# A 3x3 convolution with residual add: every engine runs in the written order, weight blocks first, packing of image n+2 ahead of the add of image n

## The chip, the cores and the metric

The kernel runs on one core of a Trainium2 chip. The metric is the device time of one execution in microseconds (us); smaller is better. Beside it stands a profile of one execution, whose span goes from the first to the last instruction that the profiler recorded on the core.

## What is computed

Sixteen images with 64 channels of 64x64 pixels are convolved with 64 filters of 64x3x3, with one pixel of zeros around each image, and a residual of the shape of the output is added. All arrays are float32.

```python
x_pad = np.pad(x, ((0, 0), (0, 0), (pad, pad), (pad, pad)), mode='constant')
for b in range(batch):
    for co in range(c_out):
        for ci in range(c_in):
            for kh in range(k):
                for kw in range(k):
                    output[b, co] += weight[co, ci, kh, kw] * x_pad[b, ci, kh:kh+h, kw:kw+w]
return (output + residual).astype(np.float32)
```

## The kernel before

**Loads.** Images are loaded in pairs (NPAIR = 8), each pair as 128 partitions (2 images x 64 channels) of 4096 pixels. `load_x(p)` (line 56) is issued by GpSimd (POOL) and converts x from float32 to bfloat16 on the way into `xr`, of which there are five buffers (NXR). The first five pairs are loaded at the start; pair p+5 is loaded when the packing has read pair p (line 100). The residual pairs go by SyncE (SP) into eight buffers `ro`, all issued at the start (line 63). The weights come by a DMA that ScalarE (ACT) issues (line 53).

**Weights.** VectorE (DVE) copies the weights once (line 72), so that they stand twice side by side; nine transposes on TensorE (PE) put them into a PSUM tile `tp` (line 76), and six copies on VectorE, which convert from float32 and are called casts here, set them as blocks into `wl` (line 88). `wl` is what every convolution matmul loads as weights.

**Packing.** Two output rows are computed at once: the 128 partitions of a packed image `xp` hold the odd rows of an image in the lower half and the even rows in the upper half. VectorE copies the even rows (line 97) and ScalarE the odd ones (line 98). There are four `xp` buffers, so the packing of an image must wait until the image four before has been convolved.

**Convolution and add.** An image takes 24 matmuls (3 kernel columns x 2 row offsets x 4 chunks of 8 row pairs, line 110), which accumulate in one PSUM tile `ps` of four banks. There are two such tiles, shared with `tp`, so image n+2 cannot start before image n has been added. Two instructions on VectorE (line 120), one for each row parity, add `ps` to the residual in `ro`, in place. When both images of a pair are done, SP stores the pair (line 123).

**What sets the order.** Each engine runs its instructions one after another in a fixed order. Here the programming framework chooses that order and sets the waits between engines; the order of the source is only its starting point. In the trace VectorE packs images 0 to 3 (line 97) before it casts the weights (line 88), although the casts stand ahead in the source, and after that it packs image n+4 after the add of image n. All DMAs share the core's 16 DMA engines; the profile lists the loads of x under queue q0, residual loads and stores under q1, the weights under q10.

Of the kernel before, what the change touches and what calls it, by code (L numbers as in the profile page):

```python
# [1 line left out]

# [5 lines left out]

FP32 = mybir.dt.float32
BF16 = mybir.dt.bfloat16  # L10
ADD = mybir.AluOpType.add


@with_exitstack
def kernel(
    ctx: ExitStack,
    tc: tile.TileContext,
    x: bass.AP,
    weight: bass.AP,
    residual: bass.AP,  # L20
    out: bass.AP,
):
    nc = tc.nc

    B, C, H, W = x.shape
    CO = weight.shape[0]
    K = weight.shape[2]
    assert C == 64 and CO == 64 and K == 3 and H == 64 and W == 64 and B == 16

    NPIX = H * W  # L30
    NPAIR = B // 2
    J = H // 2
    JC = 8
    NCHUNK = J // JC
    NXR = 5

    res_bc = residual.rearrange("b c h w -> (b c) (h w)")
    out_bc = out.rearrange("b c h w -> (b c) (h w)")
    x_bc = x.rearrange("b c h w -> (b c) (h w)")
    w_flat = weight.rearrange("co ci kh kw -> co (ci kh kw)")  # L40

    pool = ctx.enter_context(tc.tile_pool(name="pool", bufs=1))
    psum = ctx.enter_context(tc.tile_pool(name="psum", bufs=2, space=bass.MemoryType.PSUM))

    wdup = pool.tile([64, 2, 576], FP32)
    ident = pool.tile([64, 64], FP32)
    ro = [pool.tile([128, NPIX], FP32, name=f"ro{p}") for p in range(NPAIR)]
    xr = [pool.tile([128, NPIX], BF16, name=f"xr{i}") for i in range(NXR)]

    xp = [pool.tile([128, J + 1, W], BF16, name=f"xp{i}") for i in range(4)]  # L50
    wl = pool.tile([128, 2, 3, 2, 64], BF16)

    nc.scalar.dma_start(out=wdup[:, 0, :], in_=w_flat[:, :])

    def load_x(p):
        nc.gpsimd.dma_start(out=xr[p % NXR][:, :], in_=x_bc[128 * p : 128 * p + 128, :])  # L56

    load_x(0)
    make_identity(nc, ident[:, :])
    for p in range(1, NXR):  # L60
        load_x(p)
    for p in range(NPAIR):
        nc.sync.dma_start(out=ro[p][:, :], in_=res_bc[128 * p : 128 * p + 128, :])

    for t in xp:
        nc.vector.memset(t[0:64, 0, :], 0.0)  # L66
        nc.vector.memset(t[64:128, J, :], 0.0)  # L67
    nc.vector.memset(wl[0:64, 0, :, 1, :], 0.0)  # L68
    nc.vector.memset(wl[64:128, 1, :, 0, :], 0.0)  # L69


    nc.vector.tensor_copy(out=wdup[:, 1, :], in_=wdup[:, 0, :])  # L72
    wdup3 = wdup.rearrange("p d (ci t) -> p (d ci) t", t=9)
    tp = psum.tile([128, NCHUNK, JC, W], FP32, name="ps")
    for t in range(9):
        nc.tensor.transpose(out=tp[:, t // 8, t % 8, :], in_=wdup3[:, :, t], identity=ident[:, :])  # L76
    tpf = tp.rearrange("p c j w -> p (c j) w")

    for half, d, par, kh in (
        (0, 0, 0, 0),  # L80
        (1, 0, 0, 1),
        (1, 0, 1, 0),
        (0, 1, 0, 2),
        (0, 1, 1, 1),
        (1, 1, 1, 2),
    ):
        hp = slice(64 * half, 64 * half + 64)
        nc.vector.tensor_copy(out=wl[hp, d, :, par, :], in_=tpf[hp, 3 * kh : 3 * kh + 3, :])  # L88


    for p in range(NPAIR):
        o4 = ro[p].rearrange("q (j two w) -> q j two w", two=2, w=W)
        x4 = xr[p % NXR].rearrange("q (j two w) -> q j two w", two=2, w=W)
        for im in range(2):
            hp = slice(64 * im, 64 * im + 64)
            t = xp[(2 * p + im) % 4]
            nc.vector.tensor_copy(out=t[64:128, 0:J, :], in_=x4[hp, :, 0, :])  # L97
            nc.scalar.copy(out=t[0:64, 1 : J + 1, :], in_=x4[hp, :, 1, :])  # L98
        if p + NXR < NPAIR:
            load_x(p + NXR)  # L100
        for im in range(2):
            hp = slice(64 * im, 64 * im + 64)
            t = xp[(2 * p + im) % 4]
            ps = psum.tile([128, NCHUNK, JC, W], FP32, name="ps")
            order = [(1, 0), (1, 1), (0, 0), (0, 1), (2, 0), (2, 1)]
            for i, (kw, d) in enumerate(order):
                xlo, xhi = max(0, 1 - kw), min(W, W + 1 - kw)
                for c in range(NCHUNK):
                    j0 = JC * c
                    nc.tensor.matmul(  # L110
                        out=ps[:, c, :, xlo:xhi],
                        lhsT=wl[:, d, kw, :, :].rearrange("q r c -> q (r c)"),
                        rhs=t[:, j0 + d : j0 + d + JC, xlo + kw - 1 : xhi + kw - 1],
                        start=i == 0,
                        stop=i == len(order) - 1,
                        skip_group_check=True,
                    )
            psj = ps.rearrange("q c j w -> q (c j) w")
            for par in range(2):
                nc.vector.tensor_tensor(  # L120
                    out=o4[hp, :, par, :], in0=psj[64 * par : 64 * par + 64, :, :], in1=o4[hp, :, par, :], op=ADD
                )
        nc.sync.dma_start(out=out_bc[128 * p : 128 * p + 128, :], in_=ro[p][:, :])


# [1 line left out]
_INS = ['x', 'weight', 'residual']  # L127
_OUTS = [((16, 64, 64, 64), 'float32')]


# [23 lines left out]
```

## Time and profile before

| | |
|---|---|
| time, median of 3 runs | 129.42 us (128.45, 129.42 and 129.80) |
| time of the profiled execution | 128.27 us |
| its span | 126.4 us |
| mean granted TensorE clock | 0.963 |
| instructions | 994 |
| convolution matmuls, line 110 | 85.1 us busy, 377 of 384 recorded |
| adds, line 120 | 73.2 us busy, 32 of 2288 ns |
| packing, line 97 on VectorE | 11.0 us busy, 16 of 686 ns |
| packing, line 98 on ScalarE | 30.4 us busy, 16 of 1897 ns |
| casts of the weights, line 88 | 2.0 us busy, 6 of 352 ns |
| first convolution matmul | 28.66 us |
| chain that ended last | PE line 110 67%, DMA of x 19% |

The profiled execution's time is 1.87 us longer than its span; what lies around the span is outside the recorded instructions. Busy times of different engines overlap, so they don't add up to the span. "Idle before, releaser" in a row says how long the engine stood still just before that instruction, and what came last of the things it waited for. For a DMA the profile gives the time from issue to landing. A DMA queue's share is the time that its packets took, out of what 16 engines have in the span.

### The profile page before, as it was taken

The numbers are of one execution on the slowest core, as the hardware profiler recorded it, in microseconds if no ns is written. First come the engines' busy times: TensorE is split into PE (matmuls) and PEld (weight loads), VectorE is DVE, ScalarE is ACT, GpSimd is POOL, SyncE is SP. The second block draws the span as 40 slices with busy tenths as digits, with TensorE's granted clock in tenths as the row PEclk, the third lists the DMA queues.
The fourth block names the chain that finished last, engine by engine and source line by source line (L and its number), as shares of the span: only waits on it lengthen the run. The fifth ranks groups of instructions, "written<-read, shape, count | busy, mean of one in ns | idle before, by whom it ended". The sixth has DMA issues, their size and how long they took to land.

```text
span 126.4 us, 994 instructions
## 1 busy us (share of the span) xinstructions
PE 86.4 (68%) x386; PEld 38.3 (30%) x393; DVE 87.1 (69%) x65; ACT 31.6 (25%) x17; POOL 4.9 (4%) x14
## 2 busy tenths in 40 slices
PE   0003000009999999999999999999999999991000
PEld 0003000003444444444444444444444444440000
DVE  3001040063079999999999999999999989898500
ACT  4000083074060541506416144161441000000000
POOL 6300001001000010000000000000000000000000
PEclk9999999999999999999999999999999999999555
DMA  5999999999999999999999999999999999996193
GB/s 104 367 344 296 340 298 301 347 329 301 334 329 303 311 353 311 306 327 298 340 342 298 329 332 301 319 389 425 425 420 435 446 430 420 415 435 275 83 415 166
DMA packets 3540, 42.15 MB, mean 333 GB/s; under 512 B 400, under 2 KB 400, under 8 KB 464
## 3 DMA queue, kind: packets, MB, share of 16 engines
q1 hardware_dynamic: 2304, 33.56, 63.5%
q0 software_dynamic: 1152, 8.39, 31.7%
q10 hardware_dynamic: 80, 0.15, 0.3%
q8 instruction: 3, 0.05, 0.1%
q14 instruction: 1, 0.01, 0.0%
HBM read 33.70 MB, written 16.78 MB: 399 GB/s over the span
## 4 chain that ended last, share of the span: by engine, by line
PE 67%; DMA 19%; DVE 3%; DVEq 2%; issue 1%; POOL 0%; POOLq 0%
PE ps L110 67%; DMA xr<-in_x_dram 19%; DVEq L149 2%; DVE ro L120 2%; DVE xp L97 1%; DVE wl L88 1%; POOL xr L56 0%; POOL ident masks.py:197 0%; POOLq L138 0%
## 5 line engine op out<-in xcount | busy, mean ns | idle before, releaser
L110 PE MATMUL ps<-xp,wl 128*128 128x504 bf16 (+1 forms) x377 | 85.1, 384 | 16.4 <-DVE wl L88 16.0
L120 DVE TENSOR_TENSOR ro<-ps,ro 64x2048 f32<-64x2048 f32 x32 | 73.2, 2288 | 8.0 <-PE ps L110 7.5
L110 PEld LDWEIGHTS <-wl 128*128 128x128 bf16 x384 | 37.2, 99 | 64.0 <-DVE wl L88 16.4
L98 ACT COPY xp<-xr 64x2048 bf16<-64x2048 bf16 x16 | 30.4, 1897 | 62.3 <-PE ps L110 32.5
L97 DVE COPY xp<-xr 64x2048 bf16<-64x2048 bf16 x16 | 11.0, 686 | 13.7 <-DMA xr<-in_x_dram 13.5
L76 PE MATMUL ps<-ident,wdup 64*128 64x64 f32 x9 | 1.3, 320 | 11.4 <-DVE wdup L72 11.4
L72 DVE COPY wdup<-wdup 64x576 f32<-64x576 f32 x1 | 0.5, 452 | 8.7 <-DMA wdup<-in_weight_dram 8.7
L56 POOL DMA_DIRECT2D xr<-in_x_dram x8 | 4.4, 556 | 42.0 <-ACT xp L98 25.4
L76 PEld LDWEIGHTS ps<-ident,wdup 64*128 64x128 f32 x9 | 1.1, 205 | 11.4 <-issue 11.4
L88 DVE CAST wl<-ps 64x192 bf16<-64x192 f32 x6 | 2.0, 352 | 0.1
L98 ACT ACT_TABLE_LOAD x1 | 1.3, 1283 | 1.3 <-PEq L138 1.3
L66 DVE MEMSET xp<- 64x32 uint32 x4 | 0.3, 85 | 0.9 <-PEq L138 0.8
L67 DVE MEMSET xp<- 64x32 uint32 x4 | 0.3, 85 | 0.2
masks.py:199 POOL TENSOR_SCALAR_AFFINE_SELECT ident<-ident 64x64 f32<-64x64 f32 x1 | 0.3, 258 | 0.1
L69 DVE MEMSET wl<- 64x96 uint32 x1 | 0.1, 138 | 0.1
L68 DVE MEMSET wl<- 64x96 uint32 x1 | 0.1, 138 | 0.1
masks.py:197 POOL MEMSET ident<- 64x64 f32 x1 | 0.2, 170 | 0.0
L138 POOL MEMSET const-float32-0.0<- 128x1 f32 x1 | 0.1, 103 | 0.2 <-issue 0.2
L138 POOL MEMSET const-bfloat16-1.0<- 128x1 bf16 x1 | 0.1, 106 | 0.0
L138 POOL MEMSET const-uint8-127<- 128x1 uint8 x1 | 0.1, 106 | 0.0
L138 POOL MEMSET const-float32-1.0<- 128x1 f32 x1 | 0.1, 103 | 0.0
## 6 DMA issues: line engine op xcount, KB each, us to landing
ro<-in_residual_dram SPq DMA_DIRECT2D x8, 2048.0 KB, 43.2
out_dram<-ro SPq DMA_DIRECT2D x8, 2048.0 KB, 23.0
xr<-in_x_dram POOLq DMA_DIRECT2D x8, 1024.0 KB, 40.9
wdup<-in_weight_dram ACTq DMA_DIRECT2D x1, 144.0 KB, 10.1
```

Source lines behind the costliest of these rows:

```text
L56: nc.gpsimd.dma_start(out=xr[p % NXR][:, :], in_=x_bc[128 * p : 128 * p + 128, :])
L66: nc.vector.memset(t[0:64, 0, :], 0.0)
L67: nc.vector.memset(t[64:128, J, :], 0.0)
L72: nc.vector.tensor_copy(out=wdup[:, 1, :], in_=wdup[:, 0, :])
L76: nc.tensor.transpose(out=tp[:, t // 8, t % 8, :], in_=wdup3[:, :, t], identity=ident[:, :])
L88: nc.vector.tensor_copy(out=wl[hp, d, :, par, :], in_=tpf[hp, 3 * kh : 3 * kh + 3, :])
L97: nc.vector.tensor_copy(out=t[64:128, 0:J, :], in_=x4[hp, :, 0, :])
L98: nc.scalar.copy(out=t[0:64, 1 : J + 1, :], in_=x4[hp, :, 1, :])
L110: nc.tensor.matmul(out=ps[:, c, :, xlo:xhi], lhsT=wl[:, d, kw, :, :].rearrange("q r c -> q (r c)"), rhs=t[:, j0 + d : j0 + d + JC, xlo + k ...
L120: nc.vector.tensor_tensor(out=o4[hp, :, par, :], in0=psj[64 * par : 64 * par + 64, :, :], in1=o4[hp, :, par, :], op=ADD)
L138: nc = _bacc.Bacc("TRN2", target_bir_lowering=False, num_devices=1)
L149: with _tile.TileContext(nc) as tc:
```

## The change

The source is regrouped into functions, and the whole body is put under `tc.manual_schedule()`: every engine then gets its instructions in the order in which they are written. The written order is this: the loads, the zero fills, the copy, transposes and casts of the weights; then the packing of images 0 and 1; then for each image n its convolution, the packing of image n+2, and the add of image n. `load_x(p + 5)` is issued after the packing of the second image of pair p, and the store of a pair after the add of its second image. Shapes, buffers, engines and the number of instructions stay.

```diff
-    nc.scalar.dma_start(out=wdup[:, 0, :], in_=w_flat[:, :])
-
     def load_x(p):
         nc.gpsimd.dma_start(out=xr[p % NXR][:, :], in_=x_bc[128 * p : 128 * p + 128, :])
 
-    load_x(0)
-    make_identity(nc, ident[:, :])
-    for p in range(1, NXR):
-        load_x(p)
-    for p in range(NPAIR):
+    def load_ro(p):
         nc.sync.dma_start(out=ro[p][:, :], in_=res_bc[128 * p : 128 * p + 128, :])
...
+    def pack(n):
+
+        p, im = divmod(n, 2)
+        hp = slice(64 * im, 64 * im + 64)
+        x4 = xr[p % NXR].rearrange("q (j two w) -> q j two w", two=2, w=W)
+        t = xp[n % 4]
+        nc.vector.tensor_copy(out=t[64:128, 0:J, :], in_=x4[hp, :, 0, :])
+        nc.scalar.copy(out=t[0:64, 1 : J + 1, :], in_=x4[hp, :, 1, :])
+        if im == 1 and p + NXR < NPAIR:
+            load_x(p + NXR)
+
+    def convolve(n):
+        t = xp[n % 4]
+        ps = psum.tile([128, NCHUNK, JC, W], FP32, name="ps")
...
+        return ps
+
+    def add(n, ps):
+        p, im = divmod(n, 2)
+        hp = slice(64 * im, 64 * im + 64)
+        o4 = ro[p].rearrange("q (j two w) -> q j two w", two=2, w=W)
+        psj = ps.rearrange("q c j w -> q (c j) w")
+        for par in range(2):
+            nc.vector.tensor_tensor(
+                out=o4[hp, :, par, :], in0=psj[64 * par : 64 * par + 64, :, :], in1=o4[hp, :, par, :], op=ADD
+            )
+        if im == 1:
+            nc.sync.dma_start(out=out_bc[128 * p : 128 * p + 128, :], in_=ro[p][:, :])
 
+    with tc.manual_schedule():
+        nc.scalar.dma_start(out=wdup[:, 0, :], in_=w_flat[:, :])
+        load_x(0)
+        make_identity(nc, ident[:, :])
+        for p in range(1, NXR):
+            load_x(p)
+        for p in range(NPAIR):
+            load_ro(p)
...
+        nc.vector.tensor_copy(out=wdup[:, 1, :], in_=wdup[:, 0, :])
...
+        for t in range(9):
+            nc.tensor.transpose(out=tp[:, t // 8, t % 8, :], in_=wdup3[:, :, t], identity=ident[:, :])
...
+            nc.vector.tensor_copy(out=wl[hp, d, :, par, :], in_=tpf[hp, 3 * kh : 3 * kh + 3, :])
+
+        pack(0)
+        pack(1)
+        for n in range(B):
+            ps = convolve(n)
+            if n + 2 < B:
+                pack(n + 2)
+            add(n, ps)
```

The zero fills and the matmuls inside `convolve` are those of before, in the same order.

More of the change, by code (lines that the diff above doesn't have):

```diff
@@ L51 @@
     wl = pool.tile([128, 2, 3, 2, 64], BF16)
-    nc.scalar.dma_start(out=wdup[:, 0, :], in_=w_flat[:, :])
     def load_x(p):
         nc.gpsimd.dma_start(out=xr[p % NXR][:, :], in_=x_bc[128 * p : 128 * p + 128, :])
-    load_x(0)
-    make_identity(nc, ident[:, :])
-    for p in range(1, NXR):
-        load_x(p)
-    for p in range(NPAIR):
[L63 to L88, printed above, removed]
@@ L91 @@
-    for p in range(NPAIR):
-        o4 = ro[p].rearrange("q (j two w) -> q j two w", two=2, w=W)
[L93 to L123, printed above, removed]
@@ new lines, in convolve @@
+    def convolve(n):
+        t = xp[n % 4]
+        ps = psum.tile([128, NCHUNK, JC, W], FP32, name="ps")
+        order = [(1, 0), (1, 1), (0, 0), (0, 1), (2, 0), (2, 1)]
+        for i, (kw, d) in enumerate(order):
+            xlo, xhi = max(0, 1 - kw), min(W, W + 1 - kw)
+            for c in range(NCHUNK):
+                j0 = JC * c
+                nc.tensor.matmul(
+                    out=ps[:, c, :, xlo:xhi],
+                    lhsT=wl[:, d, kw, :, :].rearrange("q r c -> q (r c)"),
+                    rhs=t[:, j0 + d : j0 + d + JC, xlo + kw - 1 : xhi + kw - 1],
+                    start=i == 0,
+                    stop=i == len(order) - 1,
+                    skip_group_check=True,
+                )
+        return ps
@@ new lines, in add @@
+    def add(n, ps):
+        p, im = divmod(n, 2)
+        hp = slice(64 * im, 64 * im + 64)
+        o4 = ro[p].rearrange("q (j two w) -> q j two w", two=2, w=W)
+        psj = ps.rearrange("q c j w -> q (c j) w")
+        for par in range(2):
+            nc.vector.tensor_tensor(
+                out=o4[hp, :, par, :], in0=psj[64 * par : 64 * par + 64, :, :], in1=o4[hp, :, par, :], op=ADD
+            )
+        if im == 1:
+            nc.sync.dma_start(out=out_bc[128 * p : 128 * p + 128, :], in_=ro[p][:, :])
@@ new lines @@
+    with tc.manual_schedule():
[6 more added lines that the diff above has]
+            load_ro(p)
+        for t in xp:
+            nc.vector.memset(t[0:64, 0, :], 0.0)
+            nc.vector.memset(t[64:128, J, :], 0.0)
+        nc.vector.memset(wl[0:64, 0, :, 1, :], 0.0)
+        nc.vector.memset(wl[64:128, 1, :, 0, :], 0.0)
+        nc.vector.tensor_copy(out=wdup[:, 1, :], in_=wdup[:, 0, :])
+        wdup3 = wdup.rearrange("p d (ci t) -> p (d ci) t", t=9)
+        tp = psum.tile([128, NCHUNK, JC, W], FP32, name="ps")
+        for t in range(9):
+            nc.tensor.transpose(out=tp[:, t // 8, t % 8, :], in_=wdup3[:, :, t], identity=ident[:, :])
+        tpf = tp.rearrange("p c j w -> p (c j) w")
+        for half, d, par, kh in (
+            (0, 0, 0, 0),
+            (1, 0, 0, 1),
+            (1, 0, 1, 0),
+            (0, 1, 0, 2),
+            (0, 1, 1, 1),
+            (1, 1, 1, 2),
+        ):
+            hp = slice(64 * half, 64 * half + 64)
+            nc.vector.tensor_copy(out=wl[hp, d, :, par, :], in_=tpf[hp, 3 * kh : 3 * kh + 3, :])
[6 more added lines that the diff above has]
+            add(n, ps)
```

## The prediction

> **What bounds the kernel now.** I read the page first: engine busy times, the 40 slices, the DMA queues. No compute engine is above 69%, yet the DMA row is full from the second slice on and breaks only near the end.
>
> ```profile
> PE 86.4 (68%) x386; PEld 38.3 (30%) x393; DVE 87.1 (69%) x65; ACT 31.6 (25%) x17; POOL 4.9 (4%) x14
> DMA  5999999999999999999999999999999999996193
> q1 hardware_dynamic: 2304, 33.56, 63.5%
> q0 software_dynamic: 1152, 8.39, 31.7%
> q10 hardware_dynamic: 80, 0.15, 0.3%
> HBM read 33.70 MB, written 16.78 MB: 399 GB/s over the span
> ```
>
> Queue q0 carries x (converted to bf16 on the way: 8.39 MB are written for 16.78 MB read), q1 the residual loads and the stores. Together their packets fill 95.2% of the 16 engines' 126.4 us. The kernel is close to a stream of 50.48 MB with gaps, so the second view is the DMA queues from 5 to 81 us, while both loads run.
>
> ```profile
> q0 software_dynamic: 1102, 8.11, 50.9%
> q1 hardware_dynamic: 1109, 16.07, 50.5%
> ```
>
> The two queues share evenly. Counted as read, x is 16.22 MB, q1 16.07, the weights 0.15: 32.4 MB in 76 us, 427 GB/s. The third view is busy time by stretch (columns: stretch, length, PE, PEld, DVE, ACT, POOL, clock, DMA share, GB/s), at the end of the kernel.
>
> ```profile
> 86.00:100.00 14.00, 13.89 (x63) 6.02 (x64) 13.90 (x9) 3.79 (x2) 0.00 (x0) 1.00 1.00 430
> 114.00:115.00 1.00, 0.17 (x1) 0.00 (x0) 0.79 (x1) 0.00 (x0) 0.00 (x0) 1.00 0.95 410
> 115.00:116.00 1.00, 0.00 (x0) 0.00 (x0) 1.00 (x1) 0.00 (x0) 0.00 (x0) 1.00 0.58 246
> 116.00:117.00 1.00, 0.00 (x0) 0.00 (x0) 0.99 (x2) 0.00 (x0) 0.00 (x0) 1.00 0.19 82
> 117.00:118.00 1.00, 0.00 (x0) 0.00 (x0) 1.00 (x1) 0.00 (x0) 0.00 (x0) 0.56 0.00 0
> 118.00:119.00 1.00, 0.00 (x0) 0.00 (x0) 0.80 (x1) 0.00 (x0) 0.00 (x0) 0.50 0.00 0
> 119.00:120.00 1.00, 0.00 (x0) 0.00 (x0) 0.00 (x0) 0.00 (x0) 0.00 (x0) 0.50 0.62 262
> ```
>
> Stores alone run at the same rate (430) until about 115. Then the engines run dry until the last store is issued. Idle from 115 to 120: 0.42+0.81+1+1+0.38 = 3.6 us. That hole is all that an earlier compute chain can win from the stream. The fourth view, the timeline, shows why that chain is late (columns: start, length, engine, line, operation; in brackets the idle time before and its releaser).
>
> ```profile
> 11.41 1.26 PE L76 MATMUL ps<-ident,wdup 64*128 64x64 f32 x9 [11.41 <-DVE wdup L72]
> 16.33 3.82 ACT L98 COPY xp<-xr 64x2048 bf16<-64x2048 bf16 x2 [13.74 <-DMA xr<-in_x_dram]
> 26.17 1.41 DVE L97 COPY xp<-xr 64x2048 bf16<-64x2048 bf16 x2 [8.43 <-DMA xr<-in_x_dram]
> 27.61 2.01 DVE L88 CAST wl<-ps 64x192 bf16<-64x192 f32 x6
> 28.66 16.61 PE L110 MATMUL ps<-xp,wl 128*128 128x512 bf16 x68 [15.99 <-DVE wl L88]
> 35.59 4.59 DVE L120 TENSOR_TENSOR ro<-ps,ro 64x2048 f32<-64x2048 f32 x2 [5.96 <-PE ps L110]
> 51.48 4.59 DVE L120 TENSOR_TENSOR ro<-ps,ro 64x2048 f32<-64x2048 f32 x2
> 61.33 0.69 DVE L97 COPY xp<-xr 64x2048 bf16<-64x2048 bf16 x1
> 62.05 4.59 DVE L120 TENSOR_TENSOR ro<-ps,ro 64x2048 f32<-64x2048 f32 x2
> 103.81 4.59 DVE L120 TENSOR_TENSOR ro<-ps,ro 64x2048 f32<-64x2048 f32 x2 [0.33 <-PE ps L110]
> 114.21 4.59 DVE L120 TENSOR_TENSOR ro<-ps,ro 64x2048 f32<-64x2048 f32 x2 [0.60 <-PE ps L110]
> ```
>
> The transposes end at 12.67 and image 0 is packed by 16.33+1.91 = 18.24. But VectorE has the six weight casts behind the packing of images 2 and 3, whose x lands only at 26.17. So PE, ready from 18.24, waits 16 us in all and begins at 28.66. From there VectorE sets the pace: two adds (4.59) and a copy (0.69) make 5.28 with their gaps (62.05-51.48 = 10.57 for two images).
>
> **The change, part by part.** No instruction is added or removed, and each engine issues the same kinds and counts. Only orders differ, so every price below is a shift.
>
> *Weight casts to the front.* They run from 12.67 to 14.7, 1.6 us before x0 lands at 16.33: hidden. Were that cover gone, each us of delay would push packing by one. PE now waits for ScalarE's half of image 0 and starts at 18.25, 10.4 earlier. Image 0 takes 35.59-28.66 = 6.93 as before, so it ends at 25.2.
>
> *Packing of image n+2 ahead of the add of image n.* This adds a wait: VectorE's first add now stands behind the packing of image 2, which waits for x1 at 26.17. The add begins at 26.17+0.69+0.03 = 26.89 instead of 25.2; that is 1.7 us of the 10.4 given back. PE feels it too: image 2 needs the PSUM buffer of image 0, free at 26.89+4.59 = 31.48, where PE would be ready at 25.2+5.28 = 30.5. After that the two engines march at 5.28.
>
> Each later even packing has a due time, 0.72 ahead of its add, and its x must have landed by then. The landings are read from the issue to landing times and the timeline:
>
> ```profile
> 57.03 1.90 ACT L98 COPY xp<-xr 64x2048 bf16<-64x2048 bf16 x1 [3.94 <-DMA xr<-in_x_dram]
> 36.00 1.90 ACT L98 COPY xp<-xr 64x2048 bf16<-64x2048 bf16 x1 [6.01 <-DMA xr<-in_x_dram]
> 30.28 0.53 POOL L56 DMA_DIRECT2D xr<-in_x_dram  x1 [9.31 <-ACT xp L98]
> 46.65 0.53 POOL L56 DMA_DIRECT2D xr<-in_x_dram  x1 [15.84 <-DVE xp L97]
> xr<-in_x_dram POOLq DMA_DIRECT2D x1, 1024.0 KB, 39.4
> ```
>
> x2 lands at 36.00 and is due at 26.89+2x5.28-0.72 = 36.7; x4 at 57.03, due 57.9; x7 at 46.65+39.4 = 86.05, due 89.5. The covers are 0.7, 0.8 and 3.4 us: thin but positive, so I cost these waits at nothing. Every us lost there delays all later adds by one.
>
> *The DMAs moved with it.* POOL issues x6 after the packing of image 3 (31.5+0.7 = 32.2 instead of 30.28) and x7 after that of image 5 (about 42.8 instead of 46.65). Queue q0 still holds x3 and x4 until 57, so it never runs empty and landings stay. SP issues the stores some 8.5 us earlier, behind the residual loads in the same queue.
>
> *The end.* The add of image 13 starts at 26.89+13x5.28 = 95.5 (103.81 before). The last two are paced by PE, 114.21-103.81 = 10.40 for two: 105.9, ending at 110.5. So the last store is issued at 110.5, 8.3 us earlier than 118.8. It then lies behind the store before it:
>
> ```profile
> 93.69 4.59 DVE L120 TENSOR_TENSOR ro<-ps,ro 64x2048 f32<-64x2048 f32 x2
> 108.43 10.72 SPq L123 DMA_DIRECT2D out_dram<-ro  x2
> out_dram<-ro SPq DMA_DIRECT2D x1, 2048.0 KB, 14.5
> out_dram<-ro SPq DMA_DIRECT2D x1, 2048.0 KB, 9.2
> out_dram<-ro SPq DMA_DIRECT2D x1, 2048.0 KB, 6.3
> ```
>
> These are the landing times of the sixth, seventh and eighth store. The sixth is issued at 93.69+4.59 = 98.3 and lands at 112.8; the seventh lands at 108.43+9.2 = 117.6. A store in a full queue thus takes 4.8 to 4.9 (2.10 MB at 430 is 4.88). The last one, alone, lands at 118.8+6.3 = 125.1. Queued, it lands at 117.6+4.9 = 122.5.
>
> **The sum.** 10.4 (PE start) less 1.7 (first add behind x1) less 0.4 (pace) is 8.3 on the compute chain; of it 2.6 arrive at the end (125.1-122.5), because the stream cannot be emptied sooner. Span 126.4-2.6 = 123.8, time 128.27-2.6 = 125.7 against the profiled execution's own 128.27. The bounds of the gain: from below 1.2, if the queued store still costs its 6.3 behind 117.6; from above 3.6, the whole idle hole, if the engines that finish late catch up. A floor: 50.48 MB at 427 GB/s are 118.2 us, with 1.1 ahead of the first packet and 2.2 behind the last, a span of 121.5 and a time of 123.4. I take 4.9 since it is the spacing of stores that were queued as this one will be.
>
> The profiled execution is the lowest seen; the median shown is 129.42, and the four times together have a middle of 128.9, 0.7 above it. Half of that I carry: 126.0.
>
> By the Trainium skill, "DMA: Bandwidth & Descriptors", section "Where 436 GB/s comes from", transfers between HBM and SBUF are bound by the HBM side at about 358 GB/s. By that rule the last store would take an estimated 5.9 in the queue, the gain would be 1.6 and the profiled time 126.7. This trace disagrees: 430 GB/s for 14 us of stores.
>
> **The rivals.** *The last store costs as much queued as alone.* Then it lands at 117.6+6.3 = 123.9: gain 1.2, time 127.1 on the profiled scale, within 1%. For it speaks that the tail of the seventh store was uneven (share 0.58, then 0.19), so a slow engine may hold the last packets. Against it, the spacing of the sixth and seventh.
>
> *The compute chain sets the end.* If the stream could run faster, the store issued at 110.5 would land 6.3 later, at 116.8: gain 8.3, time 120.0. It needs the stream's remaining bytes nearly six us sooner; no stretch of the load stage beats 427 by so much. Against.
>
> *Slower: the earlier stores take x's share.* If the stores issued from 36.8 on ran beside the residual loads and not behind them, x would have a third of the stream. The five loads after x2 (10.5 MB) at 142 GB/s would take 74 us, x7 would land at 110, and the last store is issued 21.0 after x7 (110.5-89.5): 131, time 140.5. It decides from x7 at 99.1 on (time 129.6). Against it: in the trace the stores do queue behind.
>
> ```profile
> L63 SPq DMA_DIRECT2D ro<-in_residual_dram x8: 328/454/822, 0.7 to 10.9; - x8
> out_dram<-ro SPq DMA_DIRECT2D x1, 2048.0 KB, 43.0
> ro<-in_residual_dram SPq DMA_DIRECT2D x1, 2048.0 KB, 70.3
> 45.54 73.61 SPq L123 DMA_DIRECT2D out_dram<-ro  x8
> ```
>
> The first store, issued at 45.54, lands at 88.5, after the last residual load (issued 10.9, landed 81.2).
>
> **How the numbers follow.** Forecast 0.76, the store as dear as alone 0.12, compute sets the end 0.06, x starved 0.06. The time is the forecast's, 126.0. The range reaches down to the floor, 123.4, and up to 128.0: the bound of 127.1 with the 0.7 between the profiled run and the middle, rounded up. About 1% is what a measurement of this kernel can tell from no change. Faster by over 1% is the forecast, the compute rival, less a little for a forecast that runs high: 0.80; within 1%, 0.14; slower, 0.06.
>
> **What would show it.** Right: the casts directly after the transposes; the first convolution matmul near 18.3; the first add near 26.9, released by the copy behind x1; adds 5.28 apart; the last store issued between 110 and 112 and landing about 4.9 after the one before; DMA full until about 121. Wrong: an x landing that holds an add by several us in mid-kernel, stores that land ahead of residual loads, a hole in the DMA row before the last store, or a stream above 435 GB/s over long stretches.

## The result

The changed kernel takes 125.37 us (median of 4 runs, 125.34 to 125.41). The kernel before took 129.18 beside it (4 runs, 128.45 to 129.80). The ratio is 0.971, with a 95% interval of 0.965 to 0.976: 2.9% faster. In the three later comparisons below the kernel before had medians of 128.46 to 128.74, against which the gain would be nearer 2.5%. The profiled execution takes 125.34 with a span of 123.6 (before 128.27 and 126.4).

From the page of the changed kernel, the DMA slices and the two large queues (packets, MB, share of 16 engines):

```profile
DMA  5999999999999999999999999999999999999990
q1 hardware_dynamic: 2304, 33.56, 64.8%
q0 software_dynamic: 1152, 8.39, 32.4%
```

The packets and bytes are the same as before, but the hole is gone: the row is full to the second-last slice, and the shares rise because the span has shrunk around the same work (97.2% after 95.2%).

The timeline of the changed kernel (start, length, engine, line, operation, idle before and releaser):

```profile
12.52 2.02 DVE L132 CAST wl<-ps 64x192 bf16<-64x192 f32 x6 [1.41 <-PE ps L121]
16.19 3.82 ACT L66 COPY xp<-xr 64x2048 bf16<-64x2048 bf16 x2 [13.60 <-DMA xr<-in_x_dram]
18.14 12.27 PE L78 MATMUL ps<-xp,wl 128*128 128x512 bf16 x48 [5.65 <-ACT xp L66]
26.00 0.69 DVE L65 COPY xp<-xr 64x2048 bf16<-64x2048 bf16 x1 [8.40 <-DMA xr<-in_x_dram]
26.71 4.59 DVE L94 TENSOR_TENSOR ro<-ps,ro 64x2048 f32<-64x2048 f32 x2
31.45 28.82 PE L78 MATMUL ps<-xp,wl 128*128 128x512 bf16 x126 [1.04 <-DVE ro L94]
106.22 4.59 DVE L94 TENSOR_TENSOR ro<-ps,ro 64x2048 f32<-64x2048 f32 x2 [0.74 <-PE ps L78]
```

The casts run at 12.52 and PE starts at 18.14, released by ScalarE's packing, 10.5 earlier than before. The first add waits for the packing of image 2, which waits for x1 (the second pair of images). PE pays 1.04 for that at image 2. The last add ends at 110.8 (before 118.8). The issues of the last two stores, and their times to landing:

```profile
100.72 10.46 SPq L98 DMA_DIRECT2D out_dram<-ro  x2
out_dram<-ro SPq DMA_DIRECT2D x1, 2048.0 KB, 16.7
out_dram<-ro SPq DMA_DIRECT2D x1, 2048.0 KB, 11.4
```

The seventh store lands at 100.72+16.7 = 117.4, where it landed before (117.6), although it was issued 7.7 earlier: it stood in the queue. The eighth lands at 110.8+11.4 = 122.2, 4.8 after it (before 125.1). Busy time by stretch at the end (the last two columns are DMA share and GB/s):

```profile
114.00:115.00 1.00, 0.00 (x0) 0.00 (x0) 0.00 (x0) 0.00 (x0) 0.00 (x0) 0.50 1.03 442
119.00:120.00 1.00, 0.00 (x0) 0.00 (x0) 0.00 (x0) 0.00 (x0) 0.00 (x0) 0.50 0.92 393
120.00:121.00 1.00, 0.00 (x0) 0.00 (x0) 0.00 (x0) 0.00 (x0) 0.00 (x0) 0.50 0.39 164
121.00:122.00 1.00, 0.00 (x0) 0.00 (x0) 0.00 (x0) 0.00 (x0) 0.00 (x0) 0.50 0.12 49
```

All compute engines have been done since 110.8, and the stream alone runs on for 11 us. So the compute chain moved by 8.0 and the end by 2.9: the rest of the chain's gain is spent waiting for the stream.

### The profile page after: what moved, and what is told of

It is laid out like the page before. It is cut to its first block, busy times and chain, and to the rows that moved or that the text cites. A ratio compares the mean times of both kernels' runs of the same rounds, so it can differ in the third digit from the quotient of the medians.

```text
span 123.6 us, 995 instructions
## 1 busy us (share of the span) xinstructions
PE 87.9 (71%) x386; PEld 38.1 (31%) x393; DVE 87.6 (71%) x65; ACT 31.6 (26%) x17; POOL 5.0 (4%) x14
## 4 chain that ended last, share of the span: by engine, by line
PE 60%; DMA 19%; DVE 6%; DVEq 2%; issue 2%; POOL 1%; POOLq 0%
PE ps L78 60%; DMA xr<-in_x_dram 19%; DVE ro L94 6%; DVEq L166 2%; POOL xr L54 1%; POOL ident masks.py:199 0%; POOL ident masks.py:197 0%; DVE xp L65 0%; POOLq masks.py:199 0%; POOLq L155 0%
## 5 line engine op out<-in xcount | busy, mean ns | idle before, releaser
L78 PE MATMUL ps<-xp,wl 128*128 128x504 bf16 (+1 forms) x377 | 86.6, 385 | 7.1 <-ACT xp L66 5.7
L65 DVE COPY xp<-xr 64x2048 bf16<-64x2048 bf16 x16 | 11.0, 689 | 10.5 <-DMA xr<-in_x_dram 10.0
```

The lines of the kernel that those rows point to most:

```text
L78: nc.tensor.matmul(out=ps[:, c, :, xlo:xhi], lhsT=wl[:, d, kw, :, :].rearrange("q r c -> q (r c)"), rhs=t[:, j0 + d : j0 + d + JC, xlo + k ...
```

## The experiments

The theory: the weight casts at the front carry the gain, and the DMA stream caps it, as long as the last store is issued before the stream runs dry. The rivals: the packing order carries it; or the time follows the compute chain. Where a measured ratio is given, it is to the kernel before on the same chip. The changed kernel itself was timed only in the comparison above, so a difference from its 125.37 is one between comparisons; three of the kernels below that differ little from it took 125.27 to 125.42.

**The casts back behind the packing of images 0 to 3.**

```diff
-        for half, d, par, kh in (
...
-            nc.vector.tensor_copy(out=wl[hp, d, :, par, :], in_=tpf[hp, 3 * kh : 3 * kh + 3, :])
-        pack(0)
-        pack(1)
+        for n in range(4):
+            pack(n)
+        for half, d, par, kh in (
...
+            nc.vector.tensor_copy(out=wl[hp, d, :, par, :], in_=tpf[hp, 3 * kh : 3 * kh + 3, :])
         for n in range(B):
             ps = convolve(n)
-            if n + 2 < B:
+            if n >= 2 and n + 2 < B:
```

> The written order is kept, but images 0 to 3 are packed ahead of the weight casts on VectorE, as in the kernel before; from image 4 on, packing of n+2 stays ahead of the add of n. Theory (the casts carry the gain): the first convolution matmul goes back to 28.5, the first add to 35.4, the last store to about 118.6, the hole in the DMA row is there again, time 127.6 to 128.9. Rival (the packing order carries the gain): the last store is issued by 112 and the time stays at 125.3 to 126.5.

Measured: 129.66 (8 runs, 128.80 to 130.55), ratio 1.008 (1.005 to 1.012). The gain is gone, so the casts carry it. The timeline of the longest of the eight runs:

```profile
28.07 2.02 DVE L134 CAST wl<-ps 64x192 bf16<-64x192 f32 x6
29.13 87.41 PE L78 MATMUL ps<-xp,wl 128*128 128x512 bf16 x377 [15.99 <-DVE wl L134]
37.23 4.59 DVE L94 TENSOR_TENSOR ro<-ps,ro 64x2048 f32<-64x2048 f32 x2 [7.14 <-PE ps L78]
116.57 4.59 DVE L94 TENSOR_TENSOR ro<-ps,ro 64x2048 f32<-64x2048 f32 x2 [0.74 <-PE ps L78]
```

The time is longer than expected (127.6 to 128.9), with the last store at 121.2 and not 118.6 in this profile. PE starts 0.5 later than in the profile before (29.13 against 28.66). The first image takes 37.23-29.13 = 8.1 and not 6.93 (taken up below). And the adds go 5.29 apart on average (79.34 us for 15) where the kernel before had 5.24 (78.62). Where the chain sets the end, the written order thus costs some 0.7 us by these two profiles; it does not help.

**Packing four ahead, behind the add, casts at the front.**

```diff
-        pack(0)
-        pack(1)
+        for n in range(4):
+            pack(n)
         for n in range(B):
             ps = convolve(n)
-            if n + 2 < B:
-                pack(n + 2)
             add(n, ps)
+            if n + 4 < B:
+                pack(n + 4)
```

> The casts stay at the front; the packing goes back to the order that the trace of the kernel before shows: images 0 to 3 first, then image n+4 behind the add of image n. Theory (the DMA stream sets the end as long as the last store is issued before the stream runs dry at 114 to 116): the packing of image 4 waits on VectorE for x2 at 35.85 and holds the add of image 1 until 36.6, so the compute chain runs 4.4 late and the last store is issued at 115.0 to 115.6, yet the time is only 125.2 to 126.3. Rival (the time follows the compute chain): 4.4 more, 129.7.

Measured: 125.27 (4 runs, 125.10 to 126.38), ratio 0.977 (0.971 to 0.983). The time is that of the changed kernel. With this run all four combinations have been measured: with the casts at the front both packing orders gain, and with the casts late the new packing order gains nothing. The profile is of the longest of the four runs, and its compute chain is several us later. The timeline, and the clock by stretch (PE, PEld, DVE, ACT, POOL, then clock, DMA share, GB/s):

```profile
35.88 0.69 DVE L65 COPY xp<-xr 64x2048 bf16<-64x2048 bf16 x1 [3.79 <-DMA xr<-in_x_dram]
36.60 4.59 DVE L94 TENSOR_TENSOR ro<-ps,ro 64x2048 f32<-64x2048 f32 x2
41.34 70.94 PE L78 MATMUL ps<-xp,wl 128*128 128x512 bf16 x306 [3.75 <-DVE ro L94]
112.32 4.59 DVE L94 TENSOR_TENSOR ro<-ps,ro 64x2048 f32<-64x2048 f32 x2 [0.60 <-PE ps L78]
```

```profile
42.00:44.00 2.00, 2.00 (x6) 0.73 (x5) 2.00 (x1) 0.00 (x0) 0.53 (x1) 0.50 0.97 287
44.00:46.00 2.00, 2.00 (x7) 0.60 (x6) 1.99 (x2) 0.27 (x1) 0.00 (x0) 0.50 0.96 336
```

The add of image 1 begins at 36.60, as expected, behind x2. But PE, standing still for 3.75 us, comes back at half clock, which was not expected (the mean clock of this run is 0.936, of the other three 0.947 to 0.964). The last store is issued at 116.9 and not at 115.0 to 115.6, just past the point where the stream runs dry, and this run takes 126.38. So the order in which images are packed is of use after all: not for the time in itself, but because it has the last store issued at 110.8, some 4 us ahead of that point (in this run the DMA share falls to 0.54 from 115 to 116).

**Packing directly behind the add.**

```diff
-            if n + 2 < B:
-                pack(n + 2)
             add(n, ps)
+            if n + 2 < B:
+                pack(n + 2)
```

> As the changed kernel, with the packing of image n+2 directly behind the add of image n and not ahead of it. Theory (stream): the first add starts at 25.1 and no longer waits for x1, adds follow 5.3 to 5.4 apart, the last store is issued between 109 and 110.5, and the time stays at 125.2 to 125.5. Rival (the time follows the compute chain): 1 to 1.7 less, 123.6 to 124.3. Rival (the place ahead of the add is what keeps PE fed): PE waits for packing in each image, the last store after 114, time above 126.

Measured: 125.28 (4 runs, 125.12 to 125.48), ratio 0.975 (0.971 to 0.980).

```profile
25.15 4.59 DVE L94 TENSOR_TENSOR ro<-ps,ro 64x2048 f32<-64x2048 f32 x2 [7.50 <-PE ps L78]
30.61 10.57 PE L78 MATMUL ps<-xp,wl 128*128 128x512 bf16 x47 [0.30 <-DVE xp L65]
106.24 4.59 DVE L94 TENSOR_TENSOR ro<-ps,ro 64x2048 f32<-64x2048 f32 x2 [0.64 <-PE ps L78]
```

The first add no longer waits for x1 (25.15). The 1.6 us won are lost again to a wait of 0.3 on packing at every second image, so the last store is issued at 110.9, where it was, a little later than expected. The time is the same: whether the packing stands ahead of the add or behind it makes no difference to it.

**One store left out, then two, and one in the kernel before.**

```diff
-        if im == 1:
+        if im == 1 and p != 0:
             nc.sync.dma_start(out=out_bc[128 * p : 128 * p + 128, :], in_=ro[p][:, :])
```

The second has `p > 1` there; the third has `if p != 0:` ahead of the store in the kernel before.

> As the changed kernel, without the store of the first pair (2.10 MB of 50.48 MB leave the stream; the first two output images are not written). Theory (stream): the compute chain is the same, last store issued at 110.8, but the queue ahead of it is 4.9 shorter, it lands at 117.1 to 117.5, time 120.2 to 120.7. Rival (compute chain sets the end): the time stays at 125.3.

> As the changed kernel, without the stores of the first two pairs (4.19 MB less; the first four output images are not written). Theory: with one store left out the stream was just as long as the compute chain; with two the chain sets the end: last store issued at 110.8, landing 6.3 later at 117.1, time 119.9 to 120.3, so the second store left out brings 0.3 at most. Rival (the stream is still the bound): 115.2 to 115.6.

> The kernel before, without the store of the first pair (2.10 MB less in the stream; the first two output images are not written). Theory (there the compute chain sets the end and the stream waits for it): the last store is issued at 118 to 120 as before, the hole in the DMA row ahead of it grows from 3.6 to about 8.5, and the time stays in the spread of the kernel before, 127.8 to 129.8. Rival (the stream bounded the kernel before as well): 4.9 less, 123.4 to 124.4.

Measured: one store out 120.16 (4 runs), ratio 0.936 (0.932 to 0.940); two out 120.12 (2 runs, 120.10 and 120.14), ratio 0.934 (0.927 to 0.941); the kernel before with one out 128.40 (8 runs, 128.02 to 129.23), ratio 0.999 (0.996 to 1.003). In the changed kernel one store less is worth 5.2 us and the next one nothing. In the kernel before even the first is worth nothing. The stretches around the last store show why, with one store out, with two out, and in the kernel before with one out:

```profile
108.00:110.00 2.00, 0.00 (x0) 0.00 (x0) 1.99 (x2) 0.00 (x0) 0.00 (x0) 0.75 0.94 401
110.00:112.00 2.00, 0.00 (x0) 0.00 (x0) 0.92 (x1) 0.00 (x0) 0.00 (x0) 0.50 0.73 311
```

```profile
106.00:108.00 2.00, 0.40 (x2) 0.00 (x0) 1.56 (x1) 0.00 (x0) 0.00 (x0) 1.00 0.35 147
108.00:110.00 2.00, 0.00 (x0) 0.00 (x0) 1.99 (x2) 0.00 (x0) 0.00 (x0) 0.91 0.00 0
```

```profile
106.00:108.00 2.00, 2.00 (x11) 0.89 (x10) 1.99 (x2) 0.00 (x0) 0.00 (x0) 1.00 0.08 33
108.00:110.00 2.00, 2.00 (x11) 0.93 (x10) 1.39 (x2) 0.00 (x0) 0.00 (x0) 1.00 0.13 57
...
116.00:118.00 2.00, 0.00 (x0) 0.00 (x0) 1.99 (x2) 0.00 (x0) 0.00 (x0) 1.00 0.00 0
```

With one store out the stream is nearly as short as the chain (share 0.73 while the last store is issued). With two it stands idle and waits. That puts numbers to both limits: the changed kernel's compute chain alone would allow 120.1, its stream 125.4.

**Stores on a queue of their own.**

```diff
-            nc.sync.dma_start(out=out_bc[128 * p : 128 * p + 128, :], in_=ro[p][:, :])
+            nc.scalar.dma_start(out=out_bc[128 * p : 128 * p + 128, :], in_=ro[p][:, :])
```

> As the changed kernel, with the stores issued by ScalarE on its own queue instead of SyncE behind the residual loads. Theory (the slower rival of the prediction, made true: queues share the stream evenly, so x gets a third while stores and residual loads run): x3 lands near 50, x7 between 100 and 110, adds wait for it, time 132 to 140, with a stream that runs dry at the end. Rival (only the sum of bytes counts, whichever queue carries them): 125.2 to 126.

Measured: 135.78 (2 runs, 135.77 and 135.78), ratio 1.055 (1.047 to 1.063). From 45 to 80 us of this run the queues are:

```profile
q1 hardware_dynamic: 338, 5.01, 34.6%
q0 software_dynamic: 349, 2.47, 33.6%
q10 hardware_dynamic: 336, 4.98, 33.3%
```

And two rows of its timeline:

```profile
63.83 0.69 DVE L65 COPY xp<-xr 64x2048 bf16<-64x2048 bf16 x1 [4.00 <-DMA xr<-in_x_dram]
63.84 3.82 ACT L66 COPY xp<-xr 64x2048 bf16<-64x2048 bf16 x2 [10.84 <-DMA xr<-in_x_dram]
```

In the changed kernel's timeline the same packing reads:

```profile
56.25 3.82 ACT L66 COPY xp<-xr 64x2048 bf16<-64x2048 bf16 x2 [6.01 <-DMA xr<-in_x_dram]
```

The three queues, residual loads (q1), x (q0) and stores (q10), have a third each. x4 arrives at 63.8 and not at 56.25, and both packing engines wait for it, ScalarE 10.84 us and VectorE 4.00. ScalarE now also stands at each store until the add ahead of it is done, but that is not what makes x4 late: its load is issued at the start in both kernels. The same bytes cost 10.4 us more because the urgent transfer lost its share. The order in SyncE's one queue, residual loads first, keeps that from the changed kernel.

**Two queues at the start.**

```diff
         nc.scalar.dma_start(out=wdup[:, 0, :], in_=w_flat[:, :])
+        nc.scalar.dma_start(out=ro[0][:, :], in_=res_bc[0:128, :])
...
-        for p in range(NPAIR):
+        for p in range(1, NPAIR):
             load_ro(p)
```

> As the changed kernel, with the residual of the first pair issued by ScalarE behind its load of the weights, so that two queues pull at the start. Theory (the stream is the bound; from 2 to 4 us it ran at a share of 0.44 and 0.81, 0.75 us of the 16 engines): the last packets go 0.3 to 0.7 earlier, time 124.7 to 125.1; x0 may land up to 3 us later, which the compute chain's spare time covers. Rival (the start is held by the first packets' latency, not by the number of queues): 125.3 to 125.5.

Measured: 125.42 (4 runs, 125.42 to 125.53), ratio 0.974 (0.968 to 0.980). No gain. Added up over stretches of half a us from 1.5 to 5.0, both kernels moved 1.05 MB, so the slow start isn't for want of a second queue. What holds it is open. As expected, x0 landed 3 us later. The DMA row of this run, the packing of image 0, and its stores:

```profile
DMA  5999999999999999999999999999999999999792
19.31 3.82 ACT L66 COPY xp<-xr 64x2048 bf16<-64x2048 bf16 x2 [16.08 <-DMA xr<-in_x_dram]
L98 SPq DMA_DIRECT2D out_dram<-ro x8: 332/332/348, 41.6 to 115.7; - x8
DMA to landing us min/median/max: 6.6/26.3/44.1
```

The delay used up all the spare time of the compute chain: the last store is issued at 115.7, as the stream runs dry (7 in the row), and lands 6.6 later at 122.3, as against 122.2. So the time alone would not have shown a stream that was somewhat earlier. The seventh store does: it lands at 117.5 here and at 117.4 in the changed kernel.

**Zeros to keep PE going.** Two runs ask why the first image takes 6.9 in one profile and 8.1 in another. They start from the kernel with the late casts; the second has 66 in place of 60.

```diff
+        pw = psum.tile([128, NCHUNK, JC, W], FP32, name="ps")
+        for i in range(60):
+            nc.tensor.matmul(
+                out=pw[:, i % NCHUNK, :, :],
+                lhsT=warm[:, 0:2, :].rearrange("q r c -> q (r c)"),
+                rhs=warm[:, :, :],
+                start=True,
+                stop=True,
+                skip_group_check=True,
+            )
```

> As the run with the casts behind the packing of images 0 to 3, plus 60 matmuls on zeros between the transposes and the first convolution (into a free PSUM tile, from a tile of zeros; 13 to 20 us of PE in a stretch where it waited). Theory (the slow first matmuls of 427 ns, 7 in the kernel before and 13 in the run with late casts, come from PE's idle stretch, and their number is what spreads the times of a kernel that the compute chain bounds): the first image takes 5.2 to 5.6 instead of 6.9 to 8.1, time 126.6 to 127.8 with a spread under 0.6. Rival (the spread comes from the landing of x): the time stays at 128.8 to 130.5, with a spread over 1.

> As the run with 60 matmuls on zeros, with 66 of them, so that PE stands still for about 0.7 us ahead of the first convolution instead of 2.0. Theory (the slow first matmuls are the half clock after PE's idle stretch; in the ten runs with 60, three at 129.8 to 130.3 lost 1.7 to it and seven at 128.3 to 128.8 did not): the first image takes 5.2 to 5.5 from 29.9 on, the first add starts near 35.3, all runs lie within 128.2 to 128.9 and none above 129.5. Rival (the high runs have another cause, such as the landing of x): about a third of the runs above 129.5 again.

Measured with 60: 128.57 (10 runs, 128.26 to 130.31), against 126.6 to 127.8 expected, and three of the ten above 129.8. The ratios are 1.000 (0.995 to 1.005) with 60 and 0.999 (0.996 to 1.002) with 66, so neither gains over the kernel before. Two things were overlooked: the first convolution now needs the PSUM buffer that the casts read, so it starts at 29.9 and not at 29.1; and PE still stood for 2.0 us. The profiled run is the slowest of the ten; it is used here for its clock alone. The mean granted clock of the three high runs is 0.947 to 0.950, that of the seven others 0.960 to 0.973. With 66: 128.32 (10 runs, 128.18 to 128.82), none high. First the run with 60, then the run with 66:

```profile
30.00:32.00 2.00, 2.00 (x7) 0.76 (x6) 0.00 (x0) 0.19 (x1) 0.53 (x1) 0.62 1.10 336
32.00:34.00 2.00, 2.00 (x7) 0.69 (x6) 0.00 (x0) 0.00 (x0) 0.00 (x0) 0.53 0.97 295
```

```profile
30.00:32.00 2.00, 2.00 (x11) 0.88 (x9) 0.00 (x0) 0.00 (x0) 0.53 (x1) 1.00 1.08 340
32.00:34.00 2.00, 2.00 (x11) 0.92 (x10) 0.00 (x0) 0.00 (x0) 0.00 (x0) 1.00 0.98 291
```

Seven matmuls in 2 us at about half the clock, against eleven. In the run with 66 the first image takes 35.46-30.07 = 5.4. So with late casts part of the spread is how long PE stays slow after its wait: with the gap closed, the ten runs lie within 0.64 us, where late casts alone spread over 1.75.

## Why the prediction was right

**What bounds it.** Right. The load stage of the changed kernel keeps the pace (from 5 to 81 us q0 moves 8.10 MB and q1 16.14, before 8.11 and 16.07), and the hole ahead of the last store is what was won. The runs with stores left out show the chain as the limit before (0.999) and the stream after (5.2 us for 4.9 expected).

**The casts.** Right: PE starts at 18.14 (18.25 foretold), and putting the casts back takes all of the gain.

**The wait added by the packing order.** Right in place and size: the first add at 26.71 (26.89), 1.04 lost on PE at image 2 (1.0). The thin covers held; the later even packings were not held up by x.

**The last store.** Issued at 110.8 (110.5), landing at 122.2 (122.5): 4.8 behind the one before, not its 6.3 alone. The rival that it costs as much queued as alone is refuted.

**The sum.** 2.6 was foretold on the profiled executions and 2.9 came: 0.2 because the seventh store landed at 117.4 in place of 117.6, 0.1 because the spacing was 4.8. The 125.7 of the sum was nearer than the 126.0 that was given. The step that failed is the carrying over of half the distance between the profiled run and the middle of all runs. The changed kernel's runs lie within 0.07 us, those before within 1.35 in the same comparison. That spread should not have been carried. The stream, which now sets the end, does not show it; nor does a compute chain with the casts at the front, since the runs with one and two stores left out, where the chain sets the end, lie within 0.22 and 0.04. The floor of the range was also worked out with too short a start: the kernel before has no packet before 1.7 us, not 1.1, which makes the floor some 124.0 instead of 123.4. The forecast did not rest on it.

**The rivals.** The compute chain as the limit is refuted by the landing of the seventh store, which hardly moved (117.4 after 117.6) although its issue was 7.7 earlier. Its price of 120.0 was right all the same as what the chain alone would allow: the runs with stores left out took 120.1. Starving x is real, but needs a queue of its own: foretold 140.5 for a third of the stream, measured 135.8 when it was made so.

By the Trainium skill, "DMA: Bandwidth & Descriptors", section "Where 436 GB/s comes from", the HBM side binds at about 358 GB/s. The trace after disagrees as the one before did: 442 GB/s from 114 to 115 and 430 from 86 to 100, in stores alone.

## What to carry to other kernels

When one resource is full but for a hole, and its own work stays the same, the hole is about the most that any speeding up of the others can win (here a hole of 3.6 us, a chain 8.0 earlier and an end 2.9 earlier); find it in the slices before adding up what a chain saves. An engine that runs in order needs its once-only work ahead of work that waits for a transfer, even if both are small. Here the busy queues shared the DMA engines evenly (50.9% and 50.5% with two, 34.6%, 33.6% and 33.3% with three), so which queue a transfer stands in, and behind what, is a choice of priority.

## What was not expected of the hardware

PE's clock fell after short pauses. In the profiled run with 60 matmuls on zeros it stood for 2.0 us and then had 0.62 and 0.53 of its clock in the two stretches from 30 to 34; with packing four ahead, 3.75 us of standing were followed by 4 to 6 us at half clock. Seven of the ten runs with 60 showed no such loss in their times, and with the pause closed none of ten did. The length of the pause alone does not decide it. Two rows of the run with stores on their own queue, then one of the run with two queues at the start:

```profile
83.96 12.17 PE L78 MATMUL ps<-xp,wl 128*128 128x512 bf16 x47 [2.45 <-DVE ro L94]
98.73 10.68 PE L78 MATMUL ps<-xp,wl 128*128 128x512 bf16 x47 [2.60 <-DVE ro L94]
```

```profile
36.34 3.83 PE L78 MATMUL ps<-xp,wl 128*128 128x512 bf16 x17 [2.93 <-DVE ro L94]
```

After 2.45 us of standing the clock from 84 to 86 was 0.50, and the 47 recorded matmuls took 12.17 us. After 2.60 it stayed at 1.00 and as many took 10.68; after 2.93 it stayed at 1.00 too. What decides it is open. By the Trainium skill, "TensorE: Matmul & The Clock Gate", Part 1, it takes an idle window of about 3.4 us; the pauses of 2.0 and 2.45 us here are shorter.

In the kernel before, two us of the first image read:

```profile
30.00:32.00 2.00, 2.00 (x7) 0.75 (x6) 0.00 (x0) 0.00 (x0) 0.53 (x1) 1.00 1.06 307
```

The recorded clock is 1.00, yet only seven matmuls fit, as in the stretch at 0.53 above: this slow stretch, the first of the execution's convolution, does not show in that column.
